# Two transformer blocks on one core: the RWKV pair in three parts, its inverse ahead of the pair's products, bonus and gate in DRAM

## The chip, the cores and the metric

The kernel runs on one core of one Trainium2 chip. Five engines have instruction streams of their own: TensorE (PE; its weight loads are listed as PEld), VectorE (DVE), ScalarE (ACT), GpSimd (POOL) and SyncE (SP), which here issues all transfers. The metric is the device time of one execution in microseconds (us); the median of several runs counts.

## The reference

Two blocks on 1024 tokens of width 1024, in float32. The first is a gMLP and mLSTM mixer with a channel MLP; the change doesn't touch it. The second has two layers, and each layer computes

```
h = rms_norm(x);  z = h @ w_in             # columns for three branches
y = concat(rwkv7(z_a), dsa(z_b), dilated(z_c))
x = x + y @ w_out
x = x + sigmoid(rms_norm(x) @ w_gate) * (p @ w_proj)
```

The change is in the RWKV branch: six heads of width 64 with a state that is carried over all tokens,

```
sa    = state @ (-kk_t)
state = state * w_t + sa (kk_t * a_t)^T + v_t k_t^T
y_t   = state @ r_t
out   = (group_norm(y) * ln_g + ln_b + (r . k * r_k) v) * silu(g)
```

The term with r_k is the bonus, silu(g) the gate. The other branches are an attention over chosen keys (DSA, which needs a search for the 256 largest scores of each row) and three groups of dilated attention.

## The kernel before, in words

The program is written with a tile scheduler: the code lists operations, tiles and pools with a number of buffers for each tag, and the scheduler fixes the order on every engine beforehand, from priorities and its own estimate of times; buffers and waits come from the tags.

**Order of the second block.** Each layer i is worked in two halves h of 512 tokens. The calls are in2(0,0), branches(0,0), in2(0,1), branches(0,1), out2(0,0), in2(1,0), branches(1,0), out2(0,1), in2(1,1), rwkv(), branches(1,1), out2(1,0), tail2(1,1). in2 makes the inner products (dense products, L287): weights arrive as tiles wf, are split into a high part wh (ACT) and a remainder wl (POOL), three tiles deep, and go through two banks of the tag "pd". Attention has the highest priority (branches), RWKV the next (rwkv, offset 30000), dense products fill the rest.

**RWKV.** The six heads of a half are three pairs, so there are twelve pairs in all, (i, h, p), which I number 0 to 11. in2 makes the four inputs of a pair, r, k, v and g, as z tiles (L1225, tag z with eight buffers; shift, L1137 to L1140, empties the dense bank), and calls rwkv for the pair (L1227); other dense products follow (rest). A chunk has 64 tokens, a half eight chunks.

- rwkv_a (L1247) makes decays P, keys and the tile BK from the z tiles. k' (kp) overwrites the tile of k.
- rwkv_b (L1296): AR (A's side and r's side, one buffer); products (L1312): four banks, of which each gives a part of A (AD0), of XV and of YB; bonus, values and rates_values; inverse16 (L1422) stores A in DRAM (L1431), loads its 16x16 blocks (L1437), inverts them on DVE and writes them back; then the inverse of the 64x64 blocks is put together on PE (L1383 to L1419). gate and token_major stand beside it. bv overwrites r's tile, sg that of g.
- rwkv_c (L1471): the chain over eight chunks, with states in a tile SS (L1499 to L1512) and one bank "pc"; outputs (L1480) in a bank "ra"; rwkv_y (L1518): group norm, bonus, gate, and the store to yd (L1546). The last pair of all (L1493) does its outputs in two parts of four chunks, so that tail2 can begin with the first 256 tokens.

rwkv (L1548) calls rwkv_b for the pair before, rwkv_a for its own, rwkv_c for the pair before. All of them use two banks of the tag "ra"; inverse and rwkv_y share the tag lv with two buffers. prep2 (L1965) uses four tiles of tag z for p.

Of the kernel before, what the change touches and what calls it, by code (L numbers as in the profile page):

```python
# [196 lines left out]
class K:  # L197
# [824 lines left out]
    def block2(self):  # L1022
# [17 lines left out]
        self.kd = [self.dr.tile([2, 4, 128, 128], F32, name=f"kd{i}") for i in range(2)]  # L1040
        self.yd, self.ml_d, self.ud = d("yd", [8, 128, 512]), d("ml", [512, 12]), d("ud", [512, 384])
# [126 lines left out]
    def in2(self, i, h, X, xs=None):  # L1168
# [127 lines left out]
    def rwkv_b(self, i, h, p, PC, P, kk, BK, zr, kp, zv, zg):  # L1296
# [3 lines left out]
        AR = self.pr.tile([128, 8, 2, 64], F32, name="AR")  # L1300

        own, other = HEADS, HEADS[::-1]
        AD0 = tile("AD0", tag="kk")
        XV = tile("XV")
        YB = [tile(f"YB{j}") for j in range(2)]
# [4 lines left out]
        bk = BK.rearrange("p c j t -> p c (j t)")  # L1310

        def products(q):  # L1312

            c4 = slice(4 * q, 4 * q + 4)
            b4 = lambda m: m[:, None].to_broadcast([m.shape[0], 4, 64])
            for e, (y, r, o) in enumerate(zip(YB, own, other)):
                ps = self.bank("ra")
                for c in range(4):
                    nc.tensor.matmul(ps[:, c * 128:(c + 1) * 128], bk[r, 4 * q + c, 64 * e:64 * e + 128],  # L1319
                                     AR[r, 4 * q + c].rearrange("p j t -> p (j t)"), start=True, stop=True)  # L1320
                v = ps.rearrange("p (c j t) -> p j c t", c=4, j=2)
                nc.vector.tensor_tensor(c8(AD0)[r, c4], v[r, 0], b4(C["mS"][r]), op=OP.mult)
                nc.vector.tensor_tensor(c8(XV)[o, c4], v[o, 0], b4(C["mS"][o]), op=OP.mult)
                nc.vector.tensor_tensor(c8(y)[:, c4], v[:, 1], b4(C[f"mY{e}"]), op=OP.mult)

        bv, sg = zr, zg

        def bonus():
            nc.vector.scalar_tensor_tensor(bv, zr, V["rk"][:, p:p + 1], kp, op0=OP.mult, op1=OP.mult)
            ps = self.bank("ra")  # L1330
            nc.tensor.matmul(ps, C["bones"], bv, start=True, stop=True)
            nc.vector.tensor_mul(bv, ps, zv)

        def gate():
            t = self.bank("ra")
            nc.scalar.activation(t, zg, AF.Tanh, scale=0.5)
            nc.vector.scalar_tensor_tensor(sg, t, 1.0, zg, op0=OP.add, op1=OP.mult)

        def token_major(q):

            ps = self.bank("ra")
            for c in range(4):
                nc.tensor.transpose(ps[:, c * 128:(c + 1) * 128], bk[:, 4 * q + c, 0:128], self.ident)
            v = ps.rearrange("p (c h n) -> p h c n", c=4, h=2)
            c4 = slice(4 * q, 4 * q + 4)
            nc.scalar.activation(c8(KB[0])[:, c4], v[:, 0], AF.Copy, scale=C["sgn"])
            for r, o, f in zip(own, other, (-1.0, 1.0)):
                nc.scalar.activation(c8(KB[1])[o, c4], v[r, 1], AF.Copy, scale=f)

        def values():  # L1350
# [4 lines left out]
            for w, r, o in zip(W, own, other):  # L1355
                nc.scalar.activation(w[o], ps[r], AF.Copy)
# [677 lines left out]
```

## Time and profile before

| | us |
|---|---|
| median of 3 runs | 3581.43 |
| lowest, highest | 3569.78, 3581.67 |
| the profiled execution | 3562.68 |
| its span, first to last instruction | 3561.0 |
| PE, DVE, ACT, POOL busy | 3316.2, 2042.1, 1627.9, 1418.2 |
| mean granted TensorE clock | 0.944 |
| HBM traffic | 380.65 MB |

The profile is of one execution; its instructions have a time, a line of the kernel, an engine and the tiles that they write and read ("out<-in"). The chain that ended last gives 26% of the span to the dense products (L287 into "pd") and 42% to PE in all. The second block starts at about 1340 us of the span.

### The profile page before, as it was taken

Reading aid. Unit: us, or ns where it says so; the run is one execution under the profiler, and the core shown is the slowest. Engines: PE = TensorE matmul, PEld = TensorE weight load, DVE = VectorE, ACT = ScalarE, POOL = GpSimd, SP = SyncE. Lnnn points to the kernel's source line nnn. Section 1 sums busy time; section 2 is a strip of 40 time slices with the busy share of each in tenths; the row PEclk is TensorE's granted clock in tenths of the full one; section 3 lists DMA queues with packets and bytes.
Section 4 is the critical chain, followed back from the end, with each engine's and each line's share of the span. In section 5 each row is a group of like instructions: output and inputs, shape, how many; then the busy total and the mean of one; then the engine's idle time right before and its main releaser. Section 6 shows DMA issues by size and latency. Waiting matters only on the chain.

```text
span 3561.0 us, 66181 instructions
## 1 busy us (share of the span) xinstructions
PE 3316.2 (93%) x24420; PEld 2830.0 (79%) x24420; DVE 2042.1 (57%) x5855; ACT 1627.9 (46%) x3496; POOL 1418.2 (40%) x1443
## 2 busy tenths in 40 slices
PE   7989998999999997999999889999999899999977
PEld 5968787899889996786777677777878888778876
DVE  6176959111621155358569986443596359987534
ACT  3244333333423343356447654433564347674444
POOL 1333335444654454442343232234332344323355
PEclk9999998999999998998999689989999899889999
DMA  6333362223233334333423142233343333243254
GB/s 226 122 104 118 109 222 75 93 95 96 91 110 95 95 95 121 114 99 108 126 84 101 48 127 63 80 92 112 95 130 99 115 108 103 72 111 85 69 172 142
DMA packets 327460, 384.99 MB, mean 108 GB/s; under 512 B 113888, under 2 KB 189920, under 8 KB 327136
## 3 DMA queue, kind: packets, MB, share of 16 engines
q1 hardware_dynamic: 327136, 380.76, 35.2%
q8 instruction: 192, 3.15, 0.4%
q14 instruction: 132, 1.08, 0.1%
HBM read 319.73 MB, written 60.92 MB: 107 GB/s over the span
## 4 chain that ended last, share of the span: by engine, by line
PE 42%; DVE 11%; DMA 5%; ACT 2%; issue 2%; POOL 1%; SPq 0%; DVEq 0%; ACTq 0%; POOLq 0%
PE pd L287 26%; PE da L1682 1%; PE ra L1319 1%; PE db L1831 1%; PE da L1618 1%; DVE junk L1718 1%; PE da L1657 1%; PE da L1675 1%; POOL wl L255 1%; PE db L1858 1%; DMA wf<-in_w2o_dram 1%; PE da L1656 1%; DMA wf<-in_w2g_dram 1%; DMA zn<-gd 1%; PE pd L363 1%
## 5 line engine op out<-in xcount | busy, mean ns | idle before, releaser
L255 POOL TENSOR_TENSOR wl<-wf,wh 128x512 fp32r<-128x512 f32 x812 | 1081.3, 1334 | 1503.5 <-ACT wh L254 1420.2
L254 ACT ACTIVATE wh<-wf 128x512 fp32r<-128x512 f32 x812 | 508.6, 628 | 942.3 <-PE pd L287 436.2
L287 PE MATMUL pd<-wh,xh 128*128 128x256 f32 x2240 | 659.5, 297 | 21.6 <-ACT raw L567 6.6
L287 PE MATMUL pd<-wh,xl 128*128 128x256 f32 x2240 | 653.0, 292 | 6.9 <-DVE xl L1894 5.8
L287 PE MATMUL pd<-wl,xh 128*128 128x256 f32 x2240 | 651.4, 293 | 6.8 <-POOL wl L255 5.9
L287 PEld LDWEIGHTS pd<-wh,xh 128*128 128x128 f32 x2240 | 435.6, 195 | 41.0 <-issue 9.2
L287 PEld LDWEIGHTS pd<-wl,xh 128*128 128x128 f32 x2240 | 434.8, 195 | 21.3 <-POOL wl L255 9.6
L287 PEld LDWEIGHTS pd<-wh,xl 128*128 128x128 f32 x2240 | 437.3, 195 | 17.8 <-DVE xl L1894 6.6
L287 PE MATMUL pd<-xh,wh 128*128 128x512 f32 x896 | 369.7, 413 | 30.3 <-DVE tg L1148 20.4
L287 PE MATMUL pd<-xl,wh 128*128 128x512 f32 x896 | 360.7, 403 | 0.2 <-DVE xl L371 0.2
L287 PE MATMUL pd<-xh,wl 128*128 128x512 f32 x896 | 348.3, 403 | 0.1
L287 PEld LDWEIGHTS pd<-xh,wh 128*128 128x128 f32 x896 | 173.8, 194 | 75.0 <-DVE tg L1148 21.5
L1717 ACT ACTIVATE junk<-acc,t_nt 128x512 bf16<-128x512 f32 (+2 forms) x186 | 173.5, 933 | 68.7 <-DVE t_nt L1721 46.1
L287 PEld LDWEIGHTS pd<-xh,wl 128*128 128x128 f32 x896 | 172.8, 193 | 38.0 <-POOL wl L255 1.0
L287 PEld LDWEIGHTS pd<-xl,wh 128*128 128x128 f32 x896 | 173.5, 194 | 36.9 <-issue 2.2
L954 DVE CAST hh<-f 128x512 fp32r<-128x512 f32 x64 | 53.9, 842 | 244.7 <-ACT f L951 244.7
L1718 DVE TENSOR_SCALAR_CACHE_REDUCE junk<-acc,t_nt 128x384 bf16<-128x384 f32 (+2 forms) x186 | 162.8, 875 | 3.0
L1499 POOL TENSOR_SCALAR ch_z<-SS,PC 128x64 f32<-128x64 f32 x96 | 62.1, 647 | 162.4 <-DVE SS L1512 93.8
L1625 DVE SCALAR_TENSOR_TENSOR acc<-r,iw,acc 128x512 f32<-128x512 f32 (+3 forms) x140 | 104.3, 746 | 28.3 <-ACT r L1620 25.5
L287 PE MATMUL pd<-wh,hh 128*128 128x256 f32 x384 | 109.0, 284 | 3.3 <-DVE y L923 3.3
L287 PE MATMUL pa<-wl,hh 128*128 128x256 f32 x384 | 108.1, 285 | 4.2 <-POOL wl L255 4.2
L1620 ACT ACTIVATE r<-da 128x512 f32<-128x512 f32 (+3 forms) x160 | 81.2, 519 | 62.8 <-PE da L1618 52.7
(552 smaller groups left out, 7790.3 us busy)
## 6 DMA issues: line engine op xcount, KB each, us to landing
wf<-in_w_dram SPq DMA_DIRECT2D x256, 256.0 KB, 3.1
wf<-in_w2A_dram SPq DMA_DIRECT2D x144, 256.0 KB, 3.3
wf<-in_w2B_dram SPq DMA_DIRECT2D x112, 256.0 KB, 3.2
wf<-in_w_in_dram SPq DMA_DIRECT2D x80, 256.0 KB, 3.2
wf<-in_w2o_dram SPq DMA_DIRECT2D x80, 256.0 KB, 3.4
wf<-in_w2g_dram SPq DMA_DIRECT2D x80, 256.0 KB, 3.2
wa<-in_w_ada_dram SPq DMA_DIRECT2D x32, 512.0 KB, 5.3
X<-x_d SPq DMA_DIRECT2D x20, 512.0 KB, 5.9
```

The source lines that it names most:

```text
L254: nc.scalar.activation(wh, wf, AF.Copy)
L255: nc.gpsimd.tensor_sub(wl, wf, wh.bitcast(F32))
L287: self.nc.tensor.matmul(out, lhsT, rhs, start=k == first and j == 0 and q == 0, stop=k == last and j == len(bank) - 1 and q == 2)
L363: nc.tensor.transpose(ps[:, t * 128:(t + 1) * 128], x[:, k * 128:(k + 1) * 128], self.ident)
L954: nc.vector.tensor_copy(hh, f)
L1319: nc.tensor.matmul(ps[:, c * 128:(c + 1) * 128], bk[r, 4 * q + c, 64 * e:64 * e + 128], AR[r, 4 * q + c].rearrange("p j t -> p (j t)"), st ...
L1499: nc.gpsimd.tensor_scalar(zs, S_, PC[:, c:c + 1], None, op0=OP.mult)
L1618: nc.tensor.matmul(ps[:, :n], iqT[:, hd], ikT[:, s0:s0 + n], start=True, stop=True)
L1620: nc.scalar.activation(r[:, :n], ps[:, :n], AF.Relu)
L1625: nc.vector.scalar_tensor_tensor(a, r[:, :n], iw[:, hd:hd + 1], a, op0=OP.mult, op1=OP.add)
L1717: nc.scalar.activation(junk1, x1, AF.Sign, scale=-1.0, bias=nt[:, e1], accum_out=s)
L1718: ts(junk0, x0, nt[:, e0], 0.0, op0=OP.is_le, op1=OP.add, accum_out=c0[:, e0])
```

## The change

rwkv_b keeps AR and the inverse and makes A alone, in one bank with 16 products; what was beside it (products for XV and YB, values, rates_values, bonus, token_major, gate) goes into a new rwkv_v. rwkv calls rwkv_v for the pair before, rwkv_a for its own, rwkv_c for the pair before, rwkv_b for its own. AR and TT get two buffers, z tiles go from eight to seven, qT from two to one. Bonus and gate are stored in DRAM (bd) and loaded in rwkv_c. The states of the chain are written over the chunks of XV that have been used; sq, yn, y, bv and sg use W and YB instead of tag lv; the outputs and the transposes of y use "pc". The last pair's two parts are gone.

```diff
+        self.bd = d("bd", [3, 2, 128, 512])
...
-                    zt = self.pr.tile([128, 512], F32, name="z", bufs=8)
+                    zt = self.pr.tile([128, 512], F32, name="z", bufs=7)
...
-        AR = self.pr.tile([128, 8, 2, 64], F32, name="AR")
...
+        AR = self.pr.tile([128, 8, 2, 64], F32, name="AR", bufs=2)
         nc.vector.tensor_mul(AR[:, :, 0, 1:], c8(P)[:, :, 0:63], c8(kk)[:, :, 1:])
         nc.vector.tensor_copy(AR[:, :, 0, 0:1], c8(kk)[:, :, 0:1])
+        ps = self.bank("ra")
+        for c in range(8):
+            for r in HEADS:
+                nc.tensor.matmul(ps[r, c * 64:c * 64 + 64], BK[r, c, 0], AR[r, c, 0], start=True, stop=True)
         nc.vector.tensor_mul(AR[:, :, 1], c8(P), c8(zr))
...
-        for q in range(2):
-            products(q)
-        bonus()
-        values()
-        rates_values()
-        side = [gate, lambda: token_major(0), lambda: token_major(1)]
-        T, TT = tile("T", tag="P"), tile("TT")
+        AD0 = tile("AD0", tag="kk")
+        nc.vector.tensor_tensor(c8(AD0), c8(ps), C["mS"][:, None].to_broadcast([128, 8, 64]), op=OP.mult)
+        T, TT = tile("T", tag="P"), tile("TT", bufs=2)
...
         self.inverse16(AD0, T, TT)
-        for f in side:
-            f()
...
-        return i, h, p, PC, AR, XV, YB, TT, W, KB, bv, sg
+        return i, h, p, PC, AR, TT, BK, zr, kp, zv, zg
+
+    def rwkv_v(self, i, h, p, PC, AR, TT, BK, zr, kp, zv, zg):
...
+        XV = tile("XV")
+        YB = [tile(f"YB{j}") for j in range(2)]
+
+        W = [tile(f"W{j}") for j in range(2)]
+        KB = [tile("KB"), kp]
...
+        def products(q):
...
+                for c in range(4):
+                    nc.tensor.matmul(ps[:, c * 128:(c + 1) * 128], bk[r, 4 * q + c, 64 * e:64 * e + 128],
+                                     AR[r, 4 * q + c].rearrange("p j t -> p (j t)"), start=True, stop=True)
+                v = ps.rearrange("p (c j t) -> p j c t", c=4, j=2)
+                nc.vector.tensor_tensor(c8(XV)[o, c4], v[o, 0], b4(C["mS"][o]), op=OP.mult)
+                nc.vector.tensor_tensor(c8(y)[:, c4], v[:, 1], b4(C[f"mY{e}"]), op=OP.mult)
...
+        def bonus():
+            bv = zr
...
+            nc.sync.dma_start(self.bd[i, h][p, 0], bv)
+
+        def gate():
+            t = self.bank("ra")
+            nc.scalar.activation(t, zg, AF.Tanh, scale=0.5)
+            nc.vector.scalar_tensor_tensor(zg, t, 1.0, zg, op0=OP.add, op1=OP.mult)
+            nc.sync.dma_start(self.bd[i, h][p, 1], zg)
...
+        values()
+        for q in range(2):
+            products(q)
+        rates_values()
+        bonus()
+        for q in range(2):
+            token_major(q)
+        gate()
+        return i, h, p, PC, AR, XV, YB, TT, W, KB
...
-        SS = self.pr.tile([128, 512], F32, name="SS")
+        state = lambda c: XV[:, c * 64 - 64:c * 64] if c else Z
...
-            py = self.bank("ra")
...
-            if c == 3 and halves:
-                self.rwkv_y(i, h, p, outputs(0, 4), bv, sg, 0, 256, "ra")
-        self.rwkv_y(i, h, p, outputs(4 if halves else 0, 8), bv, sg, 256 if halves else 0, 512, "pc")
...
+            nc.vector.scalar_tensor_tensor(state(c + 1), pz[:, 128:192], PC[:, c:c + 1], zs, op0=OP.mult, op1=OP.add)
+        py = self.bank("pc", 1)
...
+        nc.gpsimd.tensor_copy(Z, state(8))
+
+        sq, yn, y, bv = W[0], W[1], YB[0], YB[1]
+        nc.sync.dma_start(bv, self.bd[i, h][p, 0])
...
+        sg = sq
+        nc.sync.dma_start(sg, self.bd[i, h][p, 1])
+        ps = self.bank("pc", 1)
...
-            u = self.unit and self.rwkv_b(*self.unit)
-            self.unit = self.rwkv_a(*unit) if unit else None
+            u = self.unit and self.rwkv_v(*self.unit)
+            a = unit and self.rwkv_a(*unit)
             if u:
                 self.rwkv_c(*u)
+            self.unit = self.rwkv_b(*a) if a else None
...
-        qT = pd.tile([128, 512], F32R, name="qT", bufs=2)
+        qT = pd.tile([128, 512], F32R, name="qT")
...
-            pT.append(self.split(f, [self.pr.tile([128, 512], F32R, name="z", bufs=8)[:, :n] for _ in range(2)]))
+            pT.append(self.split(f, [self.pr.tile([128, 512], F32R, name="z", bufs=7)[:, :n] for _ in range(2)]))
```

## Rows read from the trace of the kernel before

**Rows 1.** Page, part 1: busy us (share of span), instructions.

```profile
PE 3316.2 (93%) x24420; PEld 2830.0 (79%) x24420; DVE 2042.1 (57%) x5855; ACT 1627.9 (46%) x3496; POOL 1418.2 (40%) x1443
```

**Rows 2.** Windows: length, busy PE, PEld, DVE, ACT, POOL, clock, DMA; last row L287 alone.

```profile
3053.00:3121.00 68.00, 61.30 (x368) 46.96 (x367) 65.01 (x191) 40.90 (x93) 16.61 (x26) 0.70 0.22 59
3125.00:3380.00 255.00, 249.38 (x2102) 206.97 (x2102) 179.94 (x523) 137.72 (x319) 82.23 (x74) 0.95 0.32 90
3125.00:3380.00 255.00, 149.19 (x944) 127.31 (x944) 0.95 0.32 90
```

**Rows 3.** Timeline of PE, last half: start us, us, engine, line, operation, out<-in, count.

```profile
3062.19 0.39 PE L287 MATMUL pd<-xl,wh 128*128 128x512 f32 x1
3062.42 0.40 PE L287 MATMUL pd<-xh,wl 128*128 128x512 f32 x1
...
3098.27 0.77 PE L287 MATMUL pd<-xh,wh 128*128 128x512 f32 x1
...
3120.96 0.78 PE L287 MATMUL pd<-xh,wh 128*128 128x512 f32 x1
```

**Rows 4.** Timeline of ACT: the second and fourth z tile of pair 11.

```profile
3092.52 0.69 ACT L1137 ACTIVATE z<-pd,d_omu 128x512 f32<-128x512 f32 x1
...
3116.22 0.69 ACT L1137 ACTIVATE z<-pd,d_omu 128x512 f32<-128x512 f32 x1
```

**Rows 5.** Timelines of PE and DVE: end of pair 9's chain and y.

```profile
3092.17 0.31 PE L1489 MATMUL ra<-W,YB 128*64 128x64 f32 x1
...
3094.12 0.28 DVE L1512 SCALAR_TENSOR_TENSOR Z<-pc,PC,ch_z 128x64 f32<-128x64 f32 x1
...
3114.17 0.68 DVE L1545 SCALAR_TENSOR_TENSOR y<-y,z 128x512 f32<-128x512 f32 x1
```

**Rows 6.** Timelines of PE and DVE: dense work after the other gates; y(6).

```profile
1548.95 0.36 PE L287 MATMUL pd<-wh,xh 128*128 128x256 f32 x1 [0.50 <-DVE prev L1140]
...
2036.41 0.78 PE L287 MATMUL pd<-xh,wh 128*128 128x512 f32 x1
...
2525.09 0.73 DVE L1545 SCALAR_TENSOR_TENSOR y<-y,z 128x512 f32<-128x512 f32 x1
...
2540.14 0.36 PE L287 MATMUL pd<-wh,xh 128*128 128x256 f32 x1
```

**Rows 7.** Timelines of DVE and PE: pair 5's last state and its outputs.

```profile
2313.37 0.28 DVE L1512 SCALAR_TENSOR_TENSOR Z<-pc,PC,ch_z 128x64 f32<-128x64 f32 x1 [1.21 <-PE pc L1511]
...
2366.57 1.69 PE L1484 MATMUL ra<-SS,AR 64*64 64x64 f32 x32 [1.66 <-DVE kk L1283]
```

**Rows 8.** Timelines of DVE, SP and PE: pair 9 from AR to the first state.

```profile
2922.09 0.68 DVE L1306 TENSOR_TENSOR AR<-P,kk 128x504 f32<-128x504 f32 x1
...
2942.36 0.37 SPq L1431 DMA_DIRECT2D Ld<-AD  x1
...
2942.71 0.40 DVE L1324 TENSOR_TENSOR YB<-ra,masks 128x256 f32<-128x256 f32 x1
...
2990.84 0.69 PE L1416 MATMUL ra<-TT,lv 32*32 32x32 f32 x30
...
3006.25 0.28 DVE L1512 SCALAR_TENSOR_TENSOR SS<-pc,PC,ch_z 128x64 f32<-128x64 f32 x1
```

**Rows 9.** Groups by line, second block: count, busy us, mean ns, idle before and releaser.

```profile
L1354 PE MATMUL ra<-consts,z 64*64 64x64 f32 x384 | 16.7, 223 | 0.9 <-DVE t_dec L1719 0.8
```

**Rows 10.** Timelines of POOL and DVE: pair 3's BK and AR.

```profile
1812.90 0.61 POOL L1293 COPY BK<-BK 64x512 f32<-64x512 f32 x1 [7.34 <-DVE BK L1291]
...
1844.33 0.68 DVE L1306 TENSOR_TENSOR AR<-P,kk 128x504 f32<-128x504 f32 x1
```

**Rows 11.** Timelines of DVE and PE: pair 11's first y and the tail's first product.

```profile
3385.82 0.41 DVE L1545 SCALAR_TENSOR_TENSOR y<-y,z 128x256 f32<-128x256 f32 x1
...
3387.39 0.39 PE L287 MATMUL pd<-wh,xh 128*128 128x256 f32 x1
```

**Rows 12.** Line L1644 (POOL's copy into qT): what it waited for (us, times).

```profile
  PE da L1657: 24.1, 7
```

More of the change, by code (lines that the diff above doesn't have):

```diff
@@ L1308, in rwkv_b @@
+        for c in range(8):
+            for r in HEADS:
+                nc.tensor.matmul(ps[r, c * 64:c * 64 + 64], BK[r, c, 0], AR[r, c, 0], start=True, stop=True)
         nc.vector.tensor_mul(AR[:, :, 1], c8(P), c8(zr))
[L1310 to L1348, printed above, removed]
@@ L1350, in values @@
-        def values():
-            ps = self.bank("ra")
-            for c in range(8):
-                for r in HEADS:
-                    nc.tensor.matmul(ps[r, c * 64:c * 64 + 64], zv[r, c * 64:c * 64 + 64], C["cent"][r], start=True, stop=True)
-            for w, r, o in zip(W, own, other):
-                nc.scalar.activation(w[o], ps[r], AF.Copy)
-        def rates_values():
-            ps = self.bank("ra")
-            for c in range(8):
-                cs = slice(c * 64, c * 64 + 64)
-                for r, o, w in zip(own, other, W):
-                    nc.tensor.matmul(ps[r, cs], XV[o, cs], w[o, cs], start=True, stop=True)
-            nc.scalar.activation(XV, ps, AF.Copy)
@@ L1469, in inverse16, with rwkv_c @@
             nc.sync.dma_start(c8(t), full(Td[m]))
[L1471 to L1473 removed]
+    def rwkv_c(self, i, h, p, PC, AR, XV, YB, TT, W, KB):
+        nc, V = self.nc, self.v2[i]
+        col = lambda n: V[n][:, p:p + 1]
         Z = self.layer[i]["Z"][p]
[L1476 removed]
+        state = lambda c: XV[:, c * 64 - 64:c * 64] if c else Z
         small = lambda n: self.sm.tile([128, 64], F32, name=n, bufs=2)
[L1478 to L1493 removed]
         for c in range(8):
             cs = slice(c * 64, c * 64 + 64)
[L1496 removed]
+            S_ = state(c)
             zs = small("ch_z")
@@ new lines, in rwkv_c @@
+        py = self.bank("pc", 1)
+        for c in range(8):
+            for r in HEADS:
+                nc.tensor.matmul(py[r, c * 64:c * 64 + 64], AR[r, c, 1], state(c)[r], start=c == 0, stop=False)
+        for c in range(8):
+            cs = slice(c * 64, c * 64 + 64)
+            for r, w, y in zip(HEADS, W, YB):
+                nc.tensor.matmul(py[r, cs], y[:, cs], w[:, cs], start=False, stop=c == 7)
+        nc.gpsimd.tensor_copy(Z, state(8))
+        sq, yn, y, bv = W[0], W[1], YB[0], YB[1]
@@ L1536, in rwkv_y @@
-        ps = self.bank(tag, 1 if tag == "pc" else 2)[:, :n]
-        for q in range(m // 2):
+        self.rsqrt(rs, ss, 8, "c")
+        nc.vector.tensor_tensor(c8(yn), c8(py), rs[:, :, None].to_broadcast([128, 8, 64]), op=OP.mult)
+        sg = sq
+        nc.sync.dma_start(sg, self.bd[i, h][p, 1])
+        ps = self.bank("pc", 1)
+        for q in range(4):
             nc.tensor.transpose(ps[:, q * 128:(q + 1) * 128], yn[:, q * 128:(q + 1) * 128], self.ident)
-        y = tile("y")
         for o, v in zip(HEADS, ps.rearrange("p (q h t) -> h p q t", h=2, t=64)):
@@ L1640, in dsa_attend @@
         rows = slice(128 * t, 128 * t + 128)
-        qT = pd.tile([128, 512], F32R, name="qT", bufs=2)
+        qT = pd.tile([128, 512], F32R, name="qT")
         f = self.stage("q")
```

83 lines of the change are left out of this document (42 added, 41 removed).

## Prediction

> **What bounds the kernel now.** Three views, in this order. The page's first part: TensorE (PE) is busy 93% of the span [rows 1]. That share is an average, so the windows come next. In 3053 to 3121 us PE is busy at a granted clock of 0.70, going back and forth between its two levels, 1.2 and 2.4 GHz, while VectorE (DVE) is busy 65.01 of 68 us; in 3125 to 3380 the clock is 0.95 and PE is full [rows 2]. So TensorE sets the end, and it loses its time in a few stretches. The timeline tells why: the dense products (L287 into banks "pd", the filler between everything else) stop at 3062.8, come back at 3098.27, and after a second stop at 3120.96 [rows 3]. What they wait for is seen at L1137, which empties a dense bank into a tile of tag z: the second z tile of the half's last pair is written only at 3092.52, the fourth at 3116.22 [rows 4]. At 3092.5 the last output of the chain of two pairs earlier ends (the state's last products, beside it, read KB, which is a z tile), at 3114.85 the last operation on that pair's y (the last reader of its other z tiles) [rows 5]. So with eight z tiles dense work waits for **the normalised y of the pair two ahead**. Dense banks are asked for in program order, so one stuck bank stops all later dense work. I number the twelve pairs 0 to 11 as they run; the gates are then y(0), y(3), y(6), y(9), at the third pair of each half, and dense work comes back after them at 1548.95, 2036.41, 2540.14 and 3120.96 [rows 3, 6].
>
> A second order matters as much. Pair 5's last state is there at 2313.65, but its outputs start at 2366.57, released by L1283 of pair 6, the reader of a bank "ra" [rows 7]. Nothing else joins the two: banks of one tag are given out in program order. I use this rule below.
>
> **The change part by part.** I work the last half, pairs 9 to 11, and move the differences to the other three.
>
> *The inverse no longer carries the products.* Pair 9's AR is written at 2922.09; the store of A starts at 2942.36, 20.3 us later, as A is a by-product of four banks of products; the inverse's last product ends at 2991.5, and the first state is written at 3006.25 [rows 8]. After: one bank of 16 products, which the 16 of L1354 price at 16.7/12 = 1.4 us [rows 9], and one eviction; with their waits about 8 us. So 12 us are saved. But products, values and rates now stand in rwkv_v, whose banks are asked for after the inverse's. They lie open there: 18 us (AR to the last eviction is 21.0 us now [rows 8]; bounds 12 and 22). Together the first state comes **6 us later** (bounds 0 and 10).
>
> *Outputs.* They now take the single bank "pc", which the chain holds to its last state. In the kernel before they run along and end at 3092.5, 1.9 us before the last state is written at 3094.40 [rows 5]; then, they start after it and take the 1.69 us of L1484 [rows 7] and about as much for L1489, some 4 us: **6 us later**. From 3092.5 to 3114.85 the y takes 22.4 us and shares DVE with the next pair's twelve evictions of 0.40 to 0.43 us [rows 8], 5 us; I take 3 us back, bounds 0 and 6. y(9) so ends at 3114.85 + 6 + 6 - 3 = 3123.9.
>
> *The gate moves.* With seven z tiles, the fourth of pair n+2 needs one that pair n+1 gives back: the four of n+1 and the three of n+2 are all there are. That happens in rwkv_v(n+1), after the bonus. And rwkv_v(n+1) can't run ahead: W and YB have one buffer each, and y(n) uses them as sq, yn, y and bv to its end. So the gate is y(n) plus values, products and bonus: 22 us here, 18 where DVE is less full (the same 21.0 us of [rows 8] is nearest; bounds 12 and 28). The three earlier tiles come sooner, which lets as many dense products through as three weight tiles feed on one bank, 18, at 0.23 us each [rows 3]: 4 us back. **Last half: 6 + 6 - 3 + 22 - 4 = +27 us** at the gate.
>
> The Trainium skill (Perfetto Trace Analysis, Optimization Strategy) says that the same gap repeating on the engine that should be full can mean too few buffers for the next tile; by it alone one z tile fewer makes the four gaps longer, as in this sum. The rows say more, namely which release ends each gap, and zr, zv and zg are given back earlier than now: were that what counts, the sum would be the first rival's.
>
> *The other halves, by the same differences.* First: inverse and products +4, outputs +6, y -3, rwkv_v +18, -4: +21. Third: +5 +6 -3 +18 -4 = +22, of which 10 are lost, since dense work is late by itself there and comes back at 2540.14, 14 us after y(6) ended at 2525.82 [rows 6] instead of some 4: +12. Second: pair 3's BK is done at 1813.5, and its AR comes at 1844.33 [rows 10], when pair 2 leaves the one AR tile; with two it doesn't wait. Its inverse starts 31 us earlier, less 15 for the late start that the first half hands on, and rwkv_v's products lie open again, so that of +21 I leave 21 + 15 - 31 = **+5**.
>
> *How they add.* What is late by d at a gate isn't late by d at the end of the half: attention and dilated blocks go on meanwhile, and when they are done dense work has the engine alone. In 3125 to 3380 L287 has 149.19 of 255 us, 0.585 [rows 2]; I carry on that share. Second half 5, third 5 x 0.585 + 12 = 15, last 15 x 0.585 + 27 = 36, at the tail 36 x 0.585 = **21**.
>
> *Tail.* Now the first half of pair 11's y ends at 3386.2 and the tail's first product starts at 3387.39 [rows 11]. The change gives that splitting up, but y(11) should be whole before dense work is there, at 3387 + 21. The tail's second half no longer waits for a late y: **-6**, bounds 0 and -12.
>
> *TensorE.* 192 products more, for A: 16.7 us busy [rows 9]; in the starved stretches they cost nothing: **+8**, bounds 0 and 17. DVE loses 48 evictions of 64x256 and gains twelve of 128x512: 0.
>
> *DMA, SP and POOL.* 48 transfers more on SP's queue: 0.37 us of issue each [rows 8], 18 us over 2000; a store that waits for its bonus or gate holds up weight loads, and these are three tiles deep: 0, bounds 0 and 10. The reads lie behind the normalisation. With one qT tile POOL's copy waits for the attention ahead (24.1 us in 7 cases already [rows 12]), and the wl of the dense products queue behind it: **+3**, bounds 0 and 24.
>
> Sum: 21 - 6 + 8 + 3 = **+26 us** on the profiled execution's 3562.7 (span 3561.0): 3589. That execution is 0.5% under the median of the three runs, 3581.43, so the forecast for the median is 3581.4 + 26 = **3607 us**, +0.7%.
>
> **The rivals.**
> 1. *Faster: the time of the releases counts, not their number.* If the gate's tanh (it needs zg and a bank alone) runs ahead of y(n), zg(n+1) comes free early and dense work waits for the end of the chain alone: in the last half at 3094 + 6 = 3100 instead of 3121 (-21), in the second, where the chain is early by 16, some 28 + 16 = 44 us earlier than now (-44). Carried at 0.585: -44 x 0.585 = -26; (-26 x 0.585 - 21) x 0.585 = -21; less 6, plus 11: -16; with somewhat shorter waits in the other two halves -30: 3551. It decides as soon as a bank "ra" may go to a later asker. Against it: [rows 7].
> 2. *No difference.* The kernel is bound by TensorE's total; gaps shift and close elsewhere: +17 for A, -6 at the tail, 3592. For it: 93% busy. The Trainium skill (Perfetto Trace Analysis, Identifying the Most-Contended Engine) would look first at the engine with the highest occupancy, but calls matmul busy time a poor measure for TensorE; the clock of 0.70 in a stretch where PE is 90% busy agrees with the second half of that.
> 3. *Much slower: the inverse, beside the chain, slows it,* or isn't done when y(n) is. The chain of pair 9 takes 88 us for eight states [rows 5, 8]; if each waits behind three more operations of 0.68 us (as the AR's [rows 8]), that is 16 us more a chain. The gates are late by 16 more each, and pair 11's y, three chains late, holds the tail: +75 us, 3656. For it: DVE is 96% busy in the last gap [rows 2]; it decides where DVE is full. Against it: the chain stands ahead of the inverse in priority.
>
> **How the numbers follow.** Forecast 0.42 (3590 to 3630), rival 1 0.20, rival 2 0.22, rival 3 0.16. Half a per cent, 18 us, is about what a measurement of this kernel can tell from no change. Faster by more than that: rival 1 and a little beyond the forecast's low end, 0.22. Within it: rival 2 and the forecast's part under 3599, 0.28. Slower: 0.50. The range leaves out a part of rival 3 and the far end of rival 1: 3545 to 3665.
>
> **What would show it.** Right: dense work after the third pair's z tiles comes back later in the first and third half (by 15 us and more after y(0) and y(6)); the fourth z tile is written just after the bonus of the pair ahead; outputs start after the last state; AR no longer waits for the outputs of the pair ahead. Wrong: the fourth z tile ahead of that bonus (rival 1), gaps as long as now (rival 2), a chain of pair 9 over 98 us (rival 3). The forecast falls if dense work comes back at the gates no later than now.

## The result, and the profile after

The changed kernel takes **3632.48 us** in the median of four runs (3629.39 to 3639.04), the kernel before 3578.68 beside it: a ratio of 1.0157, 95% interval 1.0132 to 1.0182, or +54 us. The forecast was +26 us, 3607, in a range of 3545 to 3665. So the direction is the forecast one, and the size is twice as large.

The profiled executions lie further apart than the medians: 3639.04 us is the highest of the four runs of after, 3562.68 lower than every other run of before. Their spans differ by 76.3 us, of which 5.7 stand already ahead of the second block's first tile (1346.16 and 1351.90), in code that isn't changed. Single times below are to be read with that.

The page's first part of after (busy us, share of the span, instructions), to be held against [rows 1]:

```profile
PE 3360.6 (92%) x24804; PEld 2870.9 (79%) x24804; DVE 2044.6 (56%) x5791; ACT 1629.3 (45%) x3491; POOL 1420.0 (39%) x1455
```

VectorE (DVE), ScalarE (ACT) and POOL have as much to do as before. TensorE (PE) has 384 instructions more (the 192 products for A count as two each) and is busy 44 us longer. Little of that is the products: e1_early below has the same 24804 instructions and 3321.6 us. The rest goes with a lower granted clock, 0.925 over the span where the kernel before has 0.944 and e1_early 0.942. The windows of after show where (length, busy us of PE, PEld, DVE, ACT, POOL, granted clock, DMA share, GB/s; the last row is L287 alone):

```profile
3105.00:3199.00 94.00, 76.14 (x554) 57.46 (x554) 87.02 (x254) 58.11 (x131) 13.41 (x29) 0.60 0.19 51
3210.00:3465.00 255.00, 238.44 (x1966) 197.54 (x1966) 151.36 (x437) 113.64 (x271) 68.16 (x66) 0.91 0.32 90
3210.00:3465.00 255.00, 139.06 (x912) 120.88 (x912) 0.91 0.32 90
```

The stretch of the last half in which dense work waits was 68 us at a clock of 0.70 [rows 2]; now it is 94 us at 0.60 (means over the clock's two levels, 1.2 and 2.4 GHz). Behind it PE was full before (249.38 of 255 us, clock 0.95); now it has 238.44 at 0.91. The timelines of PE, ACT and DVE show the same stretch from near by (start us, us, engine, line, operation, out<-in), as in [rows 3 to 5] and [rows 8]:

```profile
3104.46 0.40 PE L287 MATMUL pd<-xh,wl 128*128 128x512 f32 x1
3146.34 0.31 PE L1508 MATMUL pc<-W,z 128*64 128x64 f32 x1
3153.45 0.50 PE L287 MATMUL pd<-xh,wh 128*128 128x512 f32 x1
3158.33 0.39 PE L287 MATMUL pd<-xh,wl 128*128 128x512 f32 x1
3198.43 0.79 PE L287 MATMUL pd<-xh,wh 128*128 128x512 f32 x1
...
3147.36 0.68 ACT L1138 ACTIVATE z<-pd,d_omu 128x512 f32<-128x512 f32 x1
3191.26 0.68 ACT L1138 ACTIVATE z<-pd,d_omu 128x512 f32<-128x512 f32 x1
...
2957.01 0.68 DVE L1302 TENSOR_TENSOR AR<-P,kk 128x504 f32<-128x504 f32 x1
3043.56 0.27 DVE L1509 SCALAR_TENSOR_TENSOR XV<-pc,PC,ch_z 128x64 f32<-128x64 f32 x1
3147.58 0.28 DVE L1509 SCALAR_TENSOR_TENSOR XV<-pc,PC,ch_z 128x64 f32<-128x64 f32 x1
3173.00 0.69 DVE L1539 SCALAR_TENSOR_TENSOR YB<-YB,W 128x512 f32<-128x512 f32 x1
3189.76 0.69 DVE L1404 TENSOR_TENSOR z<-ra,z 128x512 f32<-128x512 f32 x1
```

Read from the bottom: the bonus of pair 10 (L1404) ends at 3190.45, the fourth z tile of pair 11 is written from 3191.26, dense products go on at 3198.43. The third z tile (3147.36) comes in the same way behind the last products of pair 9's chain, which read a z tile (L1508, done at 3146.65). The other three halves show the same order: bonus from 1572.4, 2054.2 and 2577.6, fourth z tile from 1573.9, 2054.9 and 2579.1.

### The profile page after: what moved, and what is told of

The parts are those of the page before. It is cut to its first block, busy times and chain, and to the rows that moved or that the text cites. A ratio compares the mean times of both kernels' runs of the same rounds, so it can differ in the third digit from the quotient of the medians.

```text
span 3637.3 us, 67043 instructions
## 1 busy us (share of the span) xinstructions
PE 3360.6 (92%) x24804; PEld 2870.9 (79%) x24804; DVE 2044.6 (56%) x5791; ACT 1629.3 (45%) x3491; POOL 1420.0 (39%) x1455
## 4 chain that ended last, share of the span: by engine, by line
PE 39%; DVE 14%; DMA 5%; ACT 3%; issue 2%; POOL 1%; SPq 0%; DVEq 0%; ACTq 0%; POOLq 0%
PE pd L287 23%; PE ra L1376 1%; DVE junk L1714 1%; PE da L1678 1%; PE da L1671 1%; DVE acc L1621 1%; ACT junk L1713 1%; PE db L1827 1%; PE ra L1318 1%; PE db L1854 1%; PE da L1653 1%; POOL wl L255 1%; DMA wf<-in_w2g_dram 1%; DVE t_nt L1717 1%; PE da L1652 1%
## 5 line engine op out<-in xcount | busy, mean ns | idle before, releaser
L287 PE MATMUL pd<-wh,xh 128*128 128x256 f32 x2240 | 663.4, 298 | 35.9 <-ACT xh L1889 10.9
L287 PE MATMUL pd<-wh,xl 128*128 128x256 f32 x2240 | 662.2, 296 | 11.3 <-DVE xl L1890 11.1
L287 PE MATMUL pd<-wl,xh 128*128 128x256 f32 x2240 | 655.0, 295 | 7.8 <-POOL wl L255 7.0
L287 PEld LDWEIGHTS pd<-wh,xh 128*128 128x128 f32 x2240 | 441.7, 198 | 55.4 <-issue 14.5
L287 PEld LDWEIGHTS pd<-wh,xl 128*128 128x128 f32 x2240 | 444.1, 198 | 25.7 <-DVE xl L1890 13.5
L287 PEld LDWEIGHTS pd<-wl,xh 128*128 128x128 f32 x2240 | 441.5, 198 | 21.6 <-POOL wl L255 10.8
L287 PE MATMUL pd<-xh,wh 128*128 128x512 f32 x896 | 369.4, 413 | 33.5 <-DVE tg L1149 21.6
L287 PE MATMUL pd<-xl,wh 128*128 128x512 f32 x896 | 362.0, 404 | 0.2 <-DVE xl L371 0.2
L287 PE MATMUL pd<-xh,wl 128*128 128x512 f32 x896 | 350.9, 406 | 0.1
L287 PEld LDWEIGHTS pd<-xh,wh 128*128 128x128 f32 x896 | 174.6, 195 | 79.2 <-DVE tg L1149 22.5
L287 PEld LDWEIGHTS pd<-xh,wl 128*128 128x128 f32 x896 | 173.7, 194 | 39.9 <-issue 1.5
L287 PEld LDWEIGHTS pd<-xl,wh 128*128 128x128 f32 x896 | 174.4, 195 | 37.1 <-issue 1.8
L954 DVE CAST hh<-f 128x512 fp32r<-128x512 f32 x64 | 53.9, 842 | 244.4 <-ACT f L951 244.4
L1714 DVE TENSOR_SCALAR_CACHE_REDUCE junk<-acc,t_nt 128x384 bf16<-128x384 f32 (+2 forms) x186 | 162.8, 875 | 3.4
L1496 POOL TENSOR_SCALAR ch_z<-XV,PC 128x64 f32<-128x64 f32 x84 | 49.4, 588 | 196.6 <-DVE XV L1509 118.2
L1616 ACT ACTIVATE r<-da 128x512 f32<-128x512 f32 (+3 forms) x160 | 80.0, 518 | 72.7 <-PE da L1614 48.9
L287 PE MATMUL pa<-wl,hh 128*128 128x256 f32 x384 | 107.8, 284 | 3.8 <-POOL wl L255 3.8
L287 PE MATMUL pd<-wh,hh 128*128 128x256 f32 x384 | 108.0, 282 | 3.3 <-DVE y L923 3.3
```

The source lines that it names most:

```text
L287: self.nc.tensor.matmul(out, lhsT, rhs, start=k == first and j == 0 and q == 0, stop=k == last and j == len(bank) - 1 and q == 2)
L954: nc.vector.tensor_copy(hh, f)
L1496: nc.gpsimd.tensor_scalar(zs, S_, PC[:, c:c + 1], None, op0=OP.mult)
L1616: nc.scalar.activation(r[:, :n], ps[:, :n], AF.Relu)
L1714: ts(junk0, x0, nt[:, e0], 0.0, op0=OP.is_le, op1=OP.add, accum_out=c0[:, e0])
```

## The experiments

Ratios are to the kernel before, timed beside each, with 95% intervals; the changed kernel stands at 1.0157.

### The gate: which operation gives the last z tile back

**e1_early.** Silu(g), the function gate() of the code, moves to the end of rwkv_a, the bonus into rwkv_b ahead of the inverse; all else is as in the changed kernel, with seven z tiles.

```diff
         nc.gpsimd.tensor_copy(BK[64:, :, 2], ta[64:])
+        t = self.bank("ra")
+        nc.scalar.activation(t, zg, AF.Tanh, scale=0.5)
+        nc.vector.scalar_tensor_tensor(zg, t, 1.0, zg, op0=OP.add, op1=OP.mult)
+        nc.sync.dma_start(self.bd[i, h][p, 1], zg)
...
+        bv = zr
+        nc.vector.scalar_tensor_tensor(bv, zr, V["rk"][:, p:p + 1], kp, op0=OP.mult, op1=OP.mult)
+        ps = self.bank("ra")
+        nc.tensor.matmul(ps, C["bones"], bv, start=True, stop=True)
+        nc.vector.tensor_mul(bv, ps, zv)
+        nc.sync.dma_start(self.bd[i, h][p, 0], bv)
         T, TT = tile("T", tag="P"), tile("TT", bufs=2)
...
-        bonus()
...
-        gate()
```

> The changed kernel, but the gate (tanh, product, store) stands at the end of rwkv_a and the bonus in rwkv_b, ahead of the inverse. So g's tile and r's tile of a pair come back long before the pair ahead has its normalised y, and with seven z tiles all four of the next pair find room: one of the pair two ahead, two of the pair ahead, four of their own. Theory 1 (the loss is the wait of the fourth z tile for rwkv_v of the pair ahead, which waits for y): the gaps of 26 to 49 us that end at the bonus (last half 3105 to 3153 and 3159 to 3198) go or end at the inverse's speed, and the time falls by 45 to 80 us against the changed kernel, to 3550 to 3590. Theory 2 (the inverse beside the chain slows the chain, which is 104 us for pair 9 where it was 88): the chains stay as long, and the time falls by less than 20 us, 3612 or more. Theory 3 (more work on TensorE and a lower clock for the whole span): within 10 us of the changed kernel, 3622 to 3642.

Measured: 3580.52 us, ratio 1.0023 (1.0007 to 1.0039). Of the loss of 1.6% all but 0.2% is gone. That also rules out theory 3: the work on TensorE is the same, and the clock is back. The timelines of ACT, PE and SP of e1_early, last half:

```profile
3065.01 0.69 ACT L1138 ACTIVATE z<-pd,d_omu 128x512 f32<-128x512 f32 x1
3067.08 0.67 ACT L1138 ACTIVATE z<-pd,d_omu 128x512 f32<-128x512 f32 x1
...
3113.54 0.39 PE L287 MATMUL pd<-xh,wl 128*128 128x512 f32 x1
3154.85 0.80 PE L287 MATMUL pd<-wh,xh 128*128 128x256 f32 x2 [1.04 <-ACT xh L1883]
...
3140.90 0.42 SPq L1795 DMA_DIRECT2D dk<-kd  x1
3143.16 0.32 SPq L1679 DMA_DIRECT2D yd<-ya  x1
...
3148.57 0.32 SPq L1908 DMA_DIRECT2D yf<-yd  x1
```

The third and the fourth z tile are written one behind the other, in the middle of pair 9's chain, and no bonus or y is waited for. The wait for the last z tile is gone. But dense work is through with the inner products so much earlier that it meets the next wait: the products of out2 (released by L1883, which splits a loaded y) need y from DRAM, and its first load is issued at 3148.57, behind transfers of the dilated blocks and the attention on the same queue.

**e2_front.** gate() and bonus() stay in rwkv_v but stand first.

```diff
+        gate()
+        bonus()
         values()
...
-        bonus()
...
-        gate()
```

> The changed kernel, but gate and bonus stand first in rwkv_v, ahead of values and products. They need no tile that y of the pair ahead holds, but their banks are asked for after the inverse's. Theory 1: the fourth z tile is released at the end of the pair's inverse (3150 in the last half of the changed kernel) and not at its bonus (3190), so that dense work of the last half comes back some 35 us earlier, of the second and the first some 30; the time falls by 30 to 60 us, to 3570 to 3605. Theory 2: less than 20 us. Theory 3: within 10 us of the changed kernel.

Measured: 3594.77 us, 1.0063 (1.0039 to 1.0087), in the expected band. The row of the gate on DVE and of the fourth z tile on ACT:

```profile
3128.27 0.68 DVE L1410 SCALAR_TENSOR_TENSOR z<-ra,z 128x512 f32<-128x512 f32 x1
...
3131.95 0.69 ACT L1138 ACTIVATE z<-pd,d_omu 128x512 f32<-128x512 f32 x1 [1.53 <-DMA bd<-z]
```

The tile comes back when silu(g) has been stored, shortly ahead of the inverse's last operation (done at 3138.24) and of y (L1539, from 3154.51). Between this and the changed kernel only the order of the same calls differs.

**e3_before_z7.** The kernel before with seven z tiles.

```diff
-                    zt = self.pr.tile([128, 512], F32, name="z", bufs=8)
+                    zt = self.pr.tile([128, 512], F32, name="z", bufs=7)
```

> The kernel before with seven z tiles for eight, nothing else. There the pair two ahead holds three tiles to the end of its chain or its y and the pair ahead four, so that a new pair's first tile (with eight: its second) waits for the end of the chain, and the fourth for the values and the bonus of the pair ahead, which come about when y does (2026 and 2030 in the second half). If the number of tiles by itself is what the change loses, this costs most of its 54 us: 3615 to 3640. If what counts is which operation gives the last tile back, the cost is that of one tile's dense products let through later, up to 18 products of 0.8 us in each of four halves with a part of it made good: 8 to 30 us, 3587 to 3610. If dense work is not bound there at all: within 5 us of the kernel before.

Measured: 3590.98 us, 1.0052 (1.0036 to 1.0068): 18 us, the middle case. So in the kernel before a tile fewer costs a third of what the change loses. What it costs when tiles come back early wasn't run by itself; e1_early, with seven tiles and everything else of the change, loses 8 us in all.

### The inverse beside the chain

**e4_order.** The calls in the order of the kernel before.

```diff
-            u = self.unit and self.rwkv_v(*self.unit)
-            a = unit and self.rwkv_a(*unit)
+            u = self.unit and self.rwkv_v(*self.rwkv_b(*self.unit))
+            self.unit = self.rwkv_a(*unit) if unit else None
             if u:
                 self.rwkv_c(*u)
-            self.unit = self.rwkv_b(*a) if a else None
```

> The changed kernel with the kernel before's order of calls: a pair's inverse and rwkv_v, then the next pair's rwkv_a, then the chain, so that no inverse stands beside the chain of the pair ahead in priority. All tiles and transfers are those of the change. Theory 2 (the inverse slows the chain): the chain of pair 9 goes back from 104 to about 88 us and the time falls by 20 us or more, to 3610 or less. Theory 1: the inverse of the pair ahead, and with it rwkv_v and its bonus, comes later still, so that the gates are later: the same as the changed kernel or up to 60 us more, 3630 to 3690. Theory 3: within 10 us of the changed kernel.

Measured: 3626.61 us, 1.0152 (1.0128 to 1.0175), no difference from the changed kernel, inside what theory 3 expected and 3 us under what theory 1 did. But the edit didn't undo what it meant to: pair 10's AR is written at 3064.5, in the midst of pair 9's chain, which ends at 3135.2 and takes 101 us. With two tiles of AR and TT the data let the inverse start, whatever the order of calls. So it decides between no theories; e1_early does.

**e5_single.** e1_early with one tile of AR and one of TT, so that the data hold the inverse back.

```diff
-        AR = self.pr.tile([128, 8, 2, 64], F32, name="AR", bufs=2)
+        AR = self.pr.tile([128, 8, 2, 64], F32, name="AR")
...
-        T, TT = tile("T", tag="P"), tile("TT", bufs=2)
+        T, TT = tile("T", tag="P"), tile("TT")
```

> The kernel with the early gate and bonus (e1_early, 3580.5 us), but one tile of AR and one of TT, so that a pair's inverse again waits for the outputs of the pair ahead and can't run beside its chain. Theory 2b (where VectorE is full, its work for the inverse lengthens the chain one for one, so that the inverse off the path gains little): the chain of pair 9 goes from 115 us back to 90 to 100, the pairs follow each other by chain and inverse again, and the time stays within 15 us of e1_early, 3565 to 3596. Rival (the inverse ahead is worth what it takes off the path, some 60 us a pair, and only the gate hid that): over 30 us slower than e1_early, 3610 or more.

Measured: 3630.53 us, 1.0150 (1.0119 to 1.0180), 1.3% slower than e1_early. The chain of pair 9 on DVE (first and last state) and the first state of pair 10; first in e1_early, then in e5_single:

```profile
3008.28 0.28 DVE L1503 SCALAR_TENSOR_TENSOR XV<-pc,PC,ch_z 128x64 f32<-128x64 f32 x1
3123.30 0.28 DVE L1503 SCALAR_TENSOR_TENSOR XV<-pc,PC,ch_z 128x64 f32<-128x64 f32 x1 [0.20 <-PE pc L1502]
3181.97 0.28 DVE L1503 SCALAR_TENSOR_TENSOR XV<-pc,PC,ch_z 128x64 f32<-128x64 f32 x1
```

```profile
3043.96 0.28 DVE L1503 SCALAR_TENSOR_TENSOR XV<-pc,PC,ch_z 128x64 f32<-128x64 f32 x1
3136.15 0.28 DVE L1503 SCALAR_TENSOR_TENSOR XV<-pc,PC,ch_z 128x64 f32<-128x64 f32 x1
3241.94 0.28 DVE L1503 SCALAR_TENSOR_TENSOR XV<-pc,PC,ch_z 128x64 f32<-128x64 f32 x1
```

Half of the theory held. The chain takes 92 us where it takes 115 with the inverse beside it; over the twelve chains it is 837 us against 1027, 16 a pair. But the other half fell, and the rival had it: from pair 9's last state to pair 10's first it is 105.8 us in e5_single and 58.7 in e1_early. The inverse ahead gives 47 us there and costs 23 in the chain. So in this kernel the inverse ahead is a gain. That the late z tile hid it in the changed kernel is the likely reading, but the late tile without the inverse ahead wasn't run.

**e9_dve2.** The changed kernel with the operations of the inverse's loop on DVE done twice. They are 21 a pair and 7.3 us (L1471 to L1477), not 22 and 7.7: the expectation counted L1450 in, which isn't repeated.

```diff
-        for w in (1, 2, 4, 8):
+        for w in (1, 1, 2, 2, 4, 4, 8, 8):
```

> The changed kernel with the inverse's operations on VectorE done twice (22 operations, 7.7 us, more for each pair; the second round writes the same values). The inverse of pair 10 is done some 23 us before pair 9's y in the changed kernel, so that by itself this has room. Theory 2b (VectorE is full beside the chain, and what stands there lengthens the chain one for one): the chain of pair 9, 104 us, grows by 5 to 10 us, the last gate is that much later, and the time grows by 8 to 25 us, to 3640 to 3657. Rival (the chain is long because its steps wait for TensorE, or for something else than VectorE's work): the chain stays within 3 us and the time within 6 us of 3632.

Measured: 3690.14 us, 1.0333 (1.0302 to 1.0365): 1.7% over the changed kernel, 58 us, for 252 operations of 88 us in all; DVE's busy time grows by 68 us (2112.2 for 2044.6). The time is beyond what was expected and the way isn't the expected one. DVE, inverse and y in the changed kernel, then in e9_dve2 (first and last operation of pair 10's inverse; y of pair 9 in e9_dve2):

```profile
3096.70 0.28 DVE L1450 TENSOR_SCALAR iA<-iA 64x256 f32<-64x256 f32 x1 [0.42 <-DMA iA<-Ld]
3150.19 0.42 DVE L1352 TENSOR_SCALAR TT<-ra 32x256 f32<-32x256 f32 x1
```

```profile
3132.34 1.42 DVE L1450 TENSOR_SCALAR iA<-iA 64x256 f32<-64x256 f32 x1 [1.20 <-DMA iA<-Ld]
3217.31 0.42 DVE L1352 TENSOR_SCALAR TT<-ra 32x256 f32<-32x256 f32 x1
3208.52 0.69 DVE L1539 SCALAR_TENSOR_TENSOR YB<-YB,W 128x512 f32<-128x512 f32 x1
```

Pair 9's chain is no longer (101 us), though it has the doubled operations beside it. The inverse of pair 10 is: 85.4 us for 53.9, 31 us more for 7.3 us of work, so that it ends behind y, and the values of pair 10 are read out 6.5 us behind y where the changed kernel has 0.5.

Pair 10 is the extreme, though. From L1450 to the last L1352 the twelve inverses take 737 us for 588, 12.5 a pair. In the first and third half, where DVE is about half busy up to the gate (114.90 of 236 us and 103.37 of 221 in the changed kernel), it is 9 a pair; in the second and fourth, where it is busy 235.51 of 267 us and 233.87 of 277, it is 16. Nor is the last gate where the time goes: its bonus ends 41 us later (3231.03), but that half already begins 36 us later. The other three gates add 21, 15 and 16 us; in the first and third half the half's first inverse, which has no chain ahead of it, takes 41 and 40 us for 30.

So added work on DVE costs more where DVE is full, and which path pays for it isn't settled by the amount. "One for one, on the chain" is withdrawn; that the work costs time on one of the two paths stands.

### Terms that the forecast held small

**e6_q1** (the kernel before with one qT), **e7_prod** (the kernel before with 16 products more a pair), **e8_whole** (the kernel before, last pair's outputs in one part).

```diff
-        qT = pd.tile([128, 512], F32R, name="qT", bufs=2)
+        qT = pd.tile([128, 512], F32R, name="qT")
```

> The kernel before with one tile qT for two, nothing else. The prediction priced this at +3 us with bounds 0 and 24: 3572 to 3582 beside 3575 of the kernel before, 3599 at the upper bound. If POOL's copy, which then waits for the attention of the tile ahead, holds up the remainders of the weights queued behind it, over 10 us.

```diff
+        ps = self.bank("ra")
+        for c in range(8):
+            for r in HEADS:
+                nc.tensor.matmul(ps[r, c * 64:c * 64 + 64], BK[r, c, 0], AR[r, c, 0], start=True, stop=True)
         nc.vector.tensor_mul(AR[:, :, 1], c8(P), c8(zr))
```

> The kernel before with 16 products more for each pair, A by itself as in the change, into a bank that nobody reads (the part of A from the four banks is still what is used). It prices the second making of A: the prediction took +8 us with bounds 0 and 17. If TensorE's total work is what sets the time (theory 3): 16.7 us or more, 3589 or more. If not: 0 to 10 us.

```diff
-        halves = (i, h, p) == (1, 1, 2)
+        halves = False
```

> The kernel before with the last pair's outputs in one part, nothing else. There the first half of that pair's y ends at 3386.2 and the tail's first product starts at 3387.4; in one part its y should be whole at 3417 or a little earlier. Theory (the halves carry the tail of the kernel before): the tail starts 20 to 30 us later, the time is 12 to 25 us longer, 3587 to 3600. Rival (the tail is held by the dense products ahead of it, not by y): within 6 us of the kernel before.

Measured: qT 3583.12 us, 1.0020 (1.0002 to 1.0037), +8 us, 1 us beyond what was expected. Products 3561.46, 0.9965 (0.9952 to 0.9978), **13 us faster with more work**, which neither case expected. Outputs in one part 3581.78, 1.0016 (0.9995 to 1.0038), not told from none: there the tail's first product is 35 us later (3422.51 for 3387.39), more than the theory had, but no longer time is shown.

The second is the one to learn from. The first tile (z0, shown as z) of the second and of the third half, in e7_prod and then in the kernel before (ACT):

```profile
1778.62 0.69 ACT L1137 ACTIVATE z<-pd,d_omu 128x512 f32<-128x512 f32 x1 [1.36 <-PE pd L287]
2316.35 0.69 ACT L1137 ACTIVATE z<-pd,d_omu 128x512 f32<-128x512 f32 x1 [1.36 <-PE pd L287]
```

```profile
1769.00 0.68 ACT L1137 ACTIVATE z<-pd,d_omu 128x512 f32<-128x512 f32 x1
2336.45 0.69 ACT L1137 ACTIVATE z<-pd,d_omu 128x512 f32<-128x512 f32 x1 [1.36 <-PE pd L287]
```

The second half alone is 29.7 us shorter (537.7 for 567.5). The added products do nothing that could save time, so the gain must come from the order that the scheduler sets for everything else; why it is better there stays open. If a small edit can move this kernel by 13 us, terms of 3 to 8 us can't be measured one by one, and e6 and e8 say no more than that each is small.

### What waits next, and a version that beats both

All three stand on e1_early. **e10_y_tiles** puts y and the loaded bonus into the KB tiles and makes the products ahead of the values, **e11_act** besides gives ten half copies a pair to ACT, **e12_queue** besides issues the loads of y (L1908) from ACT.

```diff
-        sq, yn, y, bv = W[0], W[1], YB[0], YB[1]
+        sq, yn, y, bv = W[0], W[1], KB[0], KB[1]
...
-        values()
         for q in range(2):
             products(q)
+        values()
```

> The kernel with the early gate and bonus (e1_early, 3580.5 us), where y and the loaded bonus stand in the two tiles KB instead of YB, and rwkv_v makes its products ahead of its values. The products then need only that the outputs of the pair ahead are done, and run beside that pair's normalisation; behind y stand values, rates_values and the copies alone, some 8 us where e1_early has 15 to 20. Theory (with the z gate gone the pairs' own path, chain, y and rwkv_v, holds the end: in e1_early the tail waits from 3399 to 3416 for the last y, which ends at 3411): the last y comes 15 to 30 us earlier and the time falls by 8 to 17 us, to 3563 to 3573. Rival (attention and VectorE hold the halves): within 6 us of e1_early.

```diff
-            for r, w, f in zip(HEADS, W, (nc.scalar.copy, nc.vector.tensor_copy)):
+            for r, w, f in zip(HEADS, W, (nc.scalar.copy, nc.scalar.copy)):
```

(and the same for the two pairs of half copies in the inverse)

> The same as e10_y_tiles, and besides both copies of W in each step of the chain and both copies of each of two steps of the inverse go to ScalarE (ten operations a pair, 8 of 0.23 us and two of 0.43 us, 2.7 us, leave VectorE). Theory 2b: beside a full VectorE each step of the chain no longer waits in VectorE's queue for its copy; the chains in full stretches shorten by 8 us or more, the time falls by 5 to 15 us against e10_y_tiles, to 3550 to 3566, under the kernel before. Rival: two copies in a row on ScalarE cost what VectorE's queue did: within 5 us of e10_y_tiles.

```diff
-            self.nc.sync.dma_start(f, self.yd[i, h][j][:, cs])
+            self.nc.scalar.dma_start(f, self.yd[i, h][j][:, cs])
```

> The same as e11_act, but the eight loads of y in out2 (and those of the tail) are issued by ScalarE and not by SP. In e11_act dense work stops from 3115 to 3170 and from 2028 to 2062 with the z gate gone; the first load of y is issued at 3162 and 2056, right behind transfers of the dilated blocks on SP's queue that wait for results of PE and ScalarE, while the inner products that must be read out before it (the store of the last dense gate) are done at 3121 and 2035. Theory (behind the z gate the next wait is this place in SP's queue): the first load comes 15 us or more earlier in both places, the gaps shorten by as much, and the time falls by 10 to 30 us against e11_act (3573), to 3543 to 3563, under the kernel before. Rival (VectorE, which splits the loaded y, or the attention takes it back): within 6 us of e11_act.

Measured: e10 3578.38 us, 1.0015 (0.9999 to 1.0031); e11 3573.35, 0.9996 (0.9982 to 1.0011); e12 **3560.85, 0.9949 (0.9932 to 0.9966)**, faster than both kernels: 19 us under the kernel before, 2.1% under the changed one by the ratios.

e10 went by its rival: the last y ends at 3416.6 where e1_early has 3411.3, no earlier. In e11 the chains shorten as expected, pair 3's to 102.6 us from 114.1 and pair 9's to 103.0 from 112.7, but the time lies only 5 us under e10, at the low edge of the fall that was expected, and the two intervals overlap: no gain is shown. e12 got its time, but not in the way that was expected. The loads and the gaps on PE in e11_act, then in e12_queue:

```profile
3162.39 0.38 SPq L1908 DMA_DIRECT2D yf<-yd  x1
...
3115.03 0.39 PE L287 MATMUL pd<-xh,wl 128*128 128x512 f32 x1
3170.02 0.80 PE L287 MATMUL pd<-wh,xh 128*128 128x256 f32 x2
...
3421.70 0.58 PE L287 MATMUL pd<-wh,xh 128*128 128x256 f32 x1 [18.87 <-ACT xh L1883]
```

```profile
3152.34 0.33 ACTq L1908 DMA_DIRECT2D yf<-yd  x1
...
3106.14 0.39 PE L287 MATMUL pd<-xh,wl 128*128 128x512 f32 x1
3158.87 0.50 PE L287 MATMUL pd<-wh,xh 128*128 128x256 f32 x2 [0.32 <-ACT xh L1883]
...
3402.27 0.58 PE L287 MATMUL pd<-wh,xh 128*128 128x256 f32 x1 [11.22 <-ACT xh L1883]
```

The first load is 10 us earlier, not 15, and the gap is nearly as long as before, 52 us for 55; it lies 9 us earlier as a whole. The tail's first product, which is late in both, is 19 us earlier. What of the 13 us comes from the queue and what from another order of everything isn't separated.

## Why the prediction was right, and where its sizes were off

The forecast named the gate, the release that dense work waits for, and that held: the fourth z tile just behind the bonus of the pair ahead, in all four halves; outputs after the last state; AR no longer held by the outputs ahead; and with the release moved 1.3% of 1.6% are gone (e1_early). The size was half: 3632 lies midway between the forecast, 3607, and the third rival, 3656, and of that rival's sign, a chain of pair 9 over 98 us, the trace shows 104. So both were at work. That the time lies in the stated range says little, since no change would lie in it too. Term by term at the last gate, each as what it adds to the kernel before:

| term | forecast | measured | from the rows |
|---|---|---|---|
| late start of pair 9's AR | 9 | 34.9 | 2922.09 [rows 8] to 2957.01 |
| AR to first state | 6 | 2.4 | 84.2 to 86.6 |
| chain | 0 | 16.2 | 87.9 [rows 5, 8] to 104.0 |
| last state to y | 6 - 3 | 5.4 | 20.0 [rows 5] to 25.4 |
| y to dense work | 22 - 4 | 18.6 | 6.8 [rows 3, 5] to 25.4 |
| at the gate | 36 | 77.5 | 3120.96 [rows 3] to 3198.43 |

**The terms of the gate itself were about right.** Values, products and bonus behind y, less what the earlier tiles let through, came to 18.6 for 18; outputs behind the chain to 5.4 for 3; the inverse's start to 2.4 for 6.

**The chain was mis-sized: 16 us for 0.** The forecast kept this for its third rival, at three operations a state, 16 us a chain, and gave it 0.16. It decides where DVE is full, as that rival said: ahead of the gates of the first and third half, where DVE is about half busy, the chains of pairs 0 and 6 are no longer than before (72.4 us for 75.9, 72.7 for 78.7). The windows of DVE over pair 9's chain, before and then after (length, busy us and operations, granted clock, DMA share, GB/s), have 54 operations and 16.2 us of work more, and the chain is 15.9 us longer:

```profile
3006.30:3094.40 88.10, 84.65 (x227) 0.84 0.27 75
```

```profile
3043.90:3147.90 104.00, 100.84 (x281) 0.80 0.31 81
```

Pair 3 shows the same: its first state is 27.5 us earlier than before, as the second tile of AR allows, but its chain takes 105 us for 69, and the start ahead is eaten up: dense work of the second half comes back 22.7 us later where the forecast had 5. First and last state of pair 3 on DVE, after and then before:

```profile
1911.94 0.27 DVE L1509 SCALAR_TENSOR_TENSOR XV<-pc,PC,ch_z 128x64 f32<-128x64 f32 x1
2017.24 0.28 DVE L1509 SCALAR_TENSOR_TENSOR XV<-pc,PC,ch_z 128x64 f32<-128x64 f32 x1 [0.58 <-PE pc L1508]
```

```profile
1939.45 0.28 DVE L1512 SCALAR_TENSOR_TENSOR SS<-pc,PC,ch_z 128x64 f32<-128x64 f32 x1 [0.35 <-PE pc L1511]
2008.64 0.27 DVE L1512 SCALAR_TENSOR_TENSOR Z<-pc,PC,ch_z 128x64 f32<-128x64 f32 x1
```

The inverse beside it is the reason as far as e5_single shows it against e1_early, 92 us for 115. But the amount of its work isn't what counts, since doubling it left the chain of pair 9 at 101 us (e9_dve2). The argument against the rival, that the chain stands ahead of the inverse in priority, counted for little. Why is not shown; the choice of keys, which stands ahead of both, takes half of DVE's time or more beside that chain in both kernels.

**What is carried on was mis-sized: nearly all for 0.585.** Late by 27.8, 22.7, 41.8 and 77.5 us at the four gates, the next half (or the tail) begins 22.8, 24.6, 36.8 and 78.5 us late. The share itself was no bad reading, L287 has 139.06 of 255 us behind the gate for 149.19 [rows 2]. What failed is the sentence that attention goes on meanwhile. Its choice of keys does (L1714, on DVE from 3145 on); its products don't. The choice of keys, SP's queue and the attention's first product, after and then before:

```profile
3147.97 1.15 DVE L1714 TENSOR_SCALAR_CACHE_REDUCE junk<-acc,t_nt 128x896 bf16<-128x896 f32 x1
...
3203.00 3.59 SPq L251 DMA_DIRECT2D wf<-in_w2A_dram  x2
...
3219.48 2.86 SPq L251 DMA_DIRECT2D wf<-in_w2o_dram  x3
3222.39 0.90 SPq L1639 DMA_DIRECT2D q<-qd  x2
...
3232.26 0.79 PE L1652 MATMUL da<-kT,qT 128*128 128x512 f32 x1
```

```profile
3160.13 0.50 PE L1656 MATMUL da<-kT,qT 128*128 128x512 f32 x1 [0.27 <-POOL qT L1644]
```

The attention's loads of q stand on SP's queue behind loads of weights, and these wait for weight tiles that the stopped dense work holds: between 3107 and 3203 no weights are loaded. The attention also multiplies by gates that the stopped work has yet to make (gd, stored by L1150 from 3210.19). So it began 39 us after dense work came back in the kernel before and begins 34 us after it now, and with the wait gone it begins at 3120.46 (e1_early). In the first and third half it is 13 and 27 us late where the gate is 28 and 42, so there a part is made good; behind the last gate next to nothing is. Which of the two, the loads or the gates, ties it more wasn't run. The Trainium skill (Perfetto Trace Analysis, Tensor Engine Instruction) says that TensorE's queue has limited reorder: it can pull weight loads ahead of products in flight. No run here shows whether that plays a part beside SP's queue.

**The tail and the small terms** came out as held: from the last gate to the tail it is 1 us more than before, and from its first product to the end of the span 171.4 for 173.6 (forecast -6 and bounds 0 to -12). qT alone cost 8 us where the forecast had 3 (e6); A's products, for which it had 8, came with a gain of 13 (e7), so that no run shows their own cost, and the DMAs weren't measured alone.

The first rival's rule, that a bank may go to a later asker, isn't what happened, but its core was right: the time of the release counts for more than the number of tiles. The Trainium skill (Perfetto Trace Analysis, Optimization Strategy) takes repeated gaps as a hint at too few buffers. By e3_before_z7 that is 18 us here; by e1_early, with the same seven tiles and another release, all but 8 us of the loss go.

## What to carry to other kernels

When a pool loses a buffer, look for the operation that gives the deciding one back and ask what stands in front of it: here two steps that need nothing from the pair ahead (gate and bonus) were placed behind steps that do, and moving ten lines was worth 1.3%. Work taken off a serial path pays again where it lands, if the engine there is full; compare the path's length both ways before counting it as hidden. And a stop can be carried on whole if the work that was to fill the gap has its loads behind the stopped ones on one queue, or reads what the stopped work makes.

## What was not expected of the hardware

The 21 small operations of the inverse's loop, 7.3 us, made a second time (e9_dve2), lengthened the path through them by 9 us in the mean where VectorE is about half busy, by 16 where it is busy 84 to 88%, and by 31 in the worst pair, four times their own length. Likely each waits behind longer ones: between 3000 and 3125 of the changed kernel the choice of keys alone has 31 of 0.88 us. Yet a serial chain beside them on the same engine became no longer (101 us for 104). And 192 products more came with 13 us less (e7_prod), by another order of everything else.
